# The pool of small tiles moves from above to below the weights' and the large buffers' pools

## The chip, the cores and the metric

The kernel runs on one core of a Trainium2 chip. The metric is the time of one execution in microseconds (us) on the device; lower is better. Engines are named as in the profile: PE (TensorE matmuls), PEld (the weight loads of TensorE), DVE (VectorE), ACT (ScalarE), POOL (GpSimd) and SP (SyncE, which issues transfers).

## The reference

Two layers over a residual stream of 1024 tokens by 1024 features, batch 1, all in float32. Cut to what matters here:

```
for i in range(2):
    h = rms_norm(x, norm_mix_g[i])
    u_conv, q, k, v, g = split(h @ w_in[i])             # 1024 -> 3072
    conv_out = conv_module(u_conv, ...)                 # 31 taps, layer norm, silu
    ret = chunkwise_retention(q, k, v, positions)       # 4 heads of 128, chunks of 128
    ret_out = silu(g) * group_norm(ret)
    x = x + concat([conv_out, ret_out]) @ w_out[i]
    h = rms_norm(x, norm_ffn_g[i])
    x = x + square(relu(h @ w_ff1[i])) @ w_ff2[i]       # 1024 -> 4096 -> 1024
    h = rms_norm(x, norm_ple_g[i])
    x = x + sigmoid(h @ w_ple_gate[i]) * (p[i] @ w_ple_proj[i])
return rms_norm(x, final_norm_g)
```

## The kernel before, in words

Activations lie feature-major: a tile holds 128 features on the partitions and 512 tokens (half of the sequence) along the row, so a wide matmul has a stationary operand of 128x128 and a moving operand of 128x512, one PSUM bank. Each float32 operand is split into a high and a low part (`split`, lines 219 to 221: ACT rounds to the high part, DVE subtracts for the low one), and each product is three matmuls, high by high, high by low and low by high (`mm3`, lines 250 to 254). So lines 252, 253 and 254 are nearly all of PE's work, and every group of matmuls in the profile comes three times with the same count.

The stages of a layer: the input projections with the convolution, the retention and the output projection (`proj_ab` to `w_out`), in which the stationary operand is a weight tile (`w_hi`, `w_lo`) and the moving one an activation tile (`h`), or the other way round for q, k and v (`proj_tok`); the first feed-forward projection, half of it directly (`ff1_half`, line 596) and half by a seven-product scheme on sums of weights and of activations (`ff1_pair`, line 649); the second one by the same scheme (`ff2_pairs`, line 733) with a direct remainder (`ff2`, line 810); and the per-layer embedding (`ple_proj`, `ple`).

Where tiles lie is set by the order in which pools are opened (lines 77 to 95). Pools of the left side are stacked: first `const`, then in `__init__` `stage`, `w_hi`, `w_lo`, `h`, `tmp` and `small`, which stay for the whole run, and on top of them the pools of a stage, which are opened and closed in `run` with `stage_pools`: `gen`, `conv_acc`, `ret`, `ctmp`, `rtmp`, `u` (line 887), `at`, `hx`, `s_hi`, `s_lo`, `ft` (lines 951 and 952), `form`, `acc` (line 982) and `pp`, `pr` (line 991). Normalisation has its own pools on the right side, from the other end of the memory.

Bytes per partition: `stage`, `w_hi` and `w_lo` hold 2 tiles of 4096 each, `h` 8 of 8192, `tmp` 2 of 2048. The stage pools that feed matmuls have tiles of 2048, 4096 or 8192 (`u` with 2168 comes last on its stack). All these are multiples of 512. The pool `small` has ten names with three slots each; a slot is rounded up to 32 bytes, so nine names take 96 bytes each, and `gn_st` (96 bytes a slot) takes 288: 9 x 96 + 288 = 1152 bytes, which is 2 x 512 + 128.

Which operands lie where in the wide matmuls (below: "lower pools" for `stage`, `w_hi`, `w_lo`, `h`, `tmp`, "upper pools" for those of a stage):

- `h` with `w_hi`, `w_lo`: both in the lower pools (all projections, `ff1_half`, one product of five in `ff1_pair`, part of `ff2_pairs`).
- `hx` or `form` with `s_hi`, `s_lo`: both in the upper pools.
- `h` with `s_hi`, `s_lo`; `hx`, `form` or `pp` with `w_hi`, `w_lo`: one in each.

A run of `ff1_pair` is five products of four 128-row blocks, 60 matmuls, in this order: `sa` by `t2`, `sa` by `t1` (into `ps_ret`), `sb` by `t3`, `sb` by `q22`, `w` by `t4`. Here `sa`, `sb` are pairs of `s_hi`, `s_lo`; `t3` lies in `hx`, the other activation forms in `h`. There are 16 such runs in each layer. `ff2_pairs` runs 7 blocks x 4 pairs in each layer, each seven products of two 128-row blocks, 42 matmuls. The forms of the next block come back from memory by POOL's transfers (`fetch`, line 709) into a ring of slots in `h`, `hx` and `form`, each after PE has read the slot's last occupant, and are split by ACT and DVE (`ready`, line 715). At the start of a block `begin` (lines 738 to 745) computes `p` and copies it on ACT (line 744), and the next matmuls into `p` wait for that copy.

The order of each engine's instructions is the order of the program text with priorities (`background`); it does not depend on where a tile lies.

Of the kernel before, what the change touches and what calls it, by code (L numbers as in the profile page):

```python
# [72 lines left out]
class _Trunk:  # L73
    def __init__(self, ctx, tc, x, xT, pT, pos, wts, vecs, convw, tabs, outT):
        self.tc, self.nc = tc, tc.nc
        self.x_tok, self.xT, self.pT, self.pos, self.wts = x, xT, pT, pos, wts
        self.vecs, self.convw, self.tabs, self.outT = vecs, convw, tabs, outT
        pool = lambda name, bufs, **kw: ctx.enter_context(tc.tile_pool(name=name, bufs=bufs, **kw))
        psum = bass.MemoryType.PSUM
        self.const = pool("const", 1)  # L80
        self.pools = {
            "stage": pool("stage", 2),
            "w_hi": pool("w_hi", 2),
            "w_lo": pool("w_lo", 2),
            "h": pool("h", 8),
            "tmp": pool("tmp", 2),
            "small": pool("small", 3),
            "ps_mm": pool("ps_mm", 5, space=psum),
            "ps_ret": pool("ps_ret", 2, space=psum),
            "ps_aux": pool("ps_aux", 1, space=psum),  # L90
        }

        self.small([P, 1], "pad")
        self.right = ctx.enter_context(ExitStack())
        self.norm_pools()
        self.dram = pool("dram", 1, space=bass.MemoryType.DRAM)
        self.low = {}
# [987 lines left out]
```

## Time and profile before

| | |
|---|---|
| median of 3 runs | 2378.33 us (2377.74 to 2378.8) |
| time of the profiled execution | 2378.69 us |
| its span, first to last instruction | 2376.7 us |
| PE busy | 2314.1 us (97%) |
| DVE / ACT / POOL busy | 1857.8 (78%) / 1267.6 (53%) / 231.9 us (10%) |
| mean granted TensorE clock | 0.994 |

PE's records are pipelined: one matmul of 512 columns is shown for some 0.39 us, while the next starts about 0.23 us after it. So neither the busy time nor the mean duration of a matmul says how fast PE goes; the distance from one start to the next does, and it is read from the timeline of PE, or from the number of matmuls in a stretch in which PE never idles.

### The profile page before, as it was taken

What the parts mean: (1) busy time and instruction counts of PE and PEld (TensorE: products, weight loads), DVE (VectorE), ACT (ScalarE), POOL (GpSimd) and SP (SyncE); (2) the same over time, 40 slices, a digit from 0 to 9 for tenths busy, and PEclk for the clock granted to TensorE, in tenths of its full rate; (3) what the DMA queues carried; (4) which work ended last, traced back from release to release, by engine and by line L of the source; (5) the groups of instructions that cost most, each with busy time, mean ns of one, the idle gap of its engine ahead of it and who ended that gap; (6) DMA issues with size and microseconds to landing.
All of it is one profiled execution on the core that took longest, in us unless ns stands there. A gap on an engine that the chain in (4) does not pass through costs nothing.

```text
span 2376.7 us, 29537 instructions
## 1 busy us (share of the span) xinstructions
PE 2314.1 (97%) x10548; PEld 1886.0 (79%) x10548; DVE 1857.8 (78%) x3262; ACT 1267.6 (53%) x2090; POOL 231.9 (10%) x364
## 2 busy tenths in 40 slices
PE   8999999999999999999999999999999999999998
PEld 7887887778887878788888888777788877777887
DVE  8999997376666677878999889845766667777788
ACT  5335237365556676736542352464655567676454
POOL 1000011001221101000000100100022111010000
PEclk9999999999999999999999999999999999999999
DMA  7644544666666444422265454555566654343324
GB/s 271 194 160 150 172 149 163 227 199 204 219 233 239 141 151 138 155 72 88 89 195 180 149 171 156 175 196 187 191 218 233 237 194 164 126 162 120 89 80 151
DMA packets 119171, 403.29 MB, mean 170 GB/s; under 512 B 13216, under 2 KB 21408, under 8 KB 119024
## 3 DMA queue, kind: packets, MB, share of 16 engines
q1 hardware_dynamic: 64032, 220.75, 30.5%
q0 software_dynamic: 43472, 157.59, 18.6%
q10 hardware_dynamic: 11520, 23.07, 2.6%
q8 instruction: 82, 1.34, 0.2%
q14 instruction: 65, 0.53, 0.1%
HBM read 295.46 MB, written 105.91 MB: 169 GB/s over the span
## 4 chain that ended last, share of the span: by engine, by line
PE 63%; issue 20%; DVE 8%; DMA 3%; POOL 3%; ACT 3%; POOLq 0%; DVEq 0%; ACTq 0%
PE ps_mm L252 19%; PE ps_mm L253 19%; PE ps_mm L254 19%; DVE conv_acc L411 2%; PE ps_ret L252 2%; PE ps_ret L254 2%; PE ps_ret L253 2%; POOL h L712 1%; DMA stage<-in_wts_dram 1%; DVE w_lo L221 1%; DVE h L221 1%; POOL gn_rs L546 1%; DMA w_lo<-low 1%; DMA h<-forms 1%; DVE ntmp L277 0%
## 5 line engine op out<-in xcount | busy, mean ns | idle before, releaser
L252 PE MATMUL ps_mm<-h,w_hi 128*128 128x512 f32 (+1 forms) x1584 | 615.2, 388 | 8.6 <-ACT w_hi L241 4.2
L254 PE MATMUL ps_mm<-h,w_lo 128*128 128x512 f32 (+1 forms) x1584 | 611.5, 386 | 2.9 <-DMA w_lo<-low 2.7
L253 PE MATMUL ps_mm<-h,w_hi 128*128 128x512 f32 (+1 forms) x1584 | 613.0, 387 | 0.0
L220 ACT CAST w_hi<-stage 128x1024 fp32r<-128x1024 f32 (+2 forms) x240 | 226.6, 944 | 300.1 <-PE ps_mm L253 169.7
L252 PEld LDWEIGHTS ps_mm<-h,w_hi 128*128 128x128 f32 x1584 | 299.2, 189 | 69.3 <-ACT w_hi L241 6.1
L254 PEld LDWEIGHTS ps_mm<-h,w_lo 128*128 128x128 f32 x1584 | 299.3, 189 | 62.8 <-DMA w_lo<-low 3.5
L253 PEld LDWEIGHTS ps_mm<-h,w_hi 128*128 128x128 f32 x1584 | 299.6, 189 | 56.1
L411 DVE SCALAR_TENSOR_TENSOR conv_acc<-u,cw,conv_acc 128x512 f32<-128x512 f32 x480 | 334.6, 746 | 0.9
L221 DVE TENSOR_TENSOR w_lo<-stage,w_hi 128x1024 fp32r<-128x1024 f32 (+2 forms) x240 | 261.1, 1088 | 51.0 <-ACT w_hi L220 50.3
L252 PE MATMUL ps_mm<-h,s_hi 128*128 128x512 f32 x400 | 158.9, 397 | 4.5 <-ACT ps_mm L661 4.5
L253 PE MATMUL ps_mm<-h,s_hi 128*128 128x512 f32 x400 | 158.5, 396 | 0.0
L254 PE MATMUL ps_mm<-h,s_lo 128*128 128x512 f32 x400 | 158.0, 395 | 0.0
L252 PE MATMUL ps_mm<-w_hi,h 128*128 128x512 f32 x384 | 150.6, 392 | 0.0
L253 PE MATMUL ps_mm<-w_lo,h 128*128 128x512 f32 x384 | 150.3, 391 | 0.0
L254 PE MATMUL ps_mm<-w_hi,h 128*128 128x512 f32 x384 | 150.2, 391 | 0.0
L241 ACT CAST w_hi<-stage 128x1024 fp32r<-128x1024 f32 x64 | 67.5, 1054 | 154.4 <-PE ps_mm L253 80.7
L270 ACT ACTIVATE ntmp<-x 128x256 f32<-128x256 f32 x208 | 81.1, 413 | 84.7 <-DVE ntmp L277 32.2
L252 PE MATMUL ps_ret<-h,s_hi 128*128 128x512 f32 x272 | 110.0, 405 | 16.5 <-ACT ps_mm L744 14.4
L221 DVE TENSOR_TENSOR s_lo<-ft,s_hi 128x1024 fp32r<-128x1024 f32 x64 | 78.4, 1225 | 52.7 <-ACT s_hi L220 52.7
L221 DVE TENSOR_TENSOR h<-h 128x1024 fp32r<-128x1024 f32 x76 | 92.6, 1222 | 30.8 <-ACT h L220 30.4
L254 PE MATMUL ps_ret<-h,s_lo 128*128 128x512 f32 x272 | 108.4, 398 | 0.0
L253 PE MATMUL ps_ret<-h,s_hi 128*128 128x512 f32 x272 | 108.0, 397 | 0.0
(267 smaller groups left out, 4310.1 us busy)
## 6 DMA issues: line engine op xcount, KB each, us to landing
stage<-in_wts_dram SPq DMA_DIRECT2D x336, 512.0 KB, 4.2
forms<-ft POOLq DMA_DIRECT2D x88, 512.0 KB, 6.2
low<-w_lo POOLq DMA_DIRECT2D x64, 512.0 KB, 5.2
w_lo<-low SPq DMA_DIRECT2D x64, 512.0 KB, 3.3
h<-forms POOLq DMA_DIRECT2D x62, 512.0 KB, 6.0
early<-at ACTq DMA_DIRECT2D x32, 512.0 KB, 4.4
at<-early POOLq DMA_DIRECT2D x30, 512.0 KB, 4.2
hx<-forms POOLq DMA_DIRECT2D x18, 512.0 KB, 5.7
```

What stands on the lines that cost most here:

```text
L220: self.nc.scalar.copy(hi, src)
L221: self.nc.vector.tensor_sub(lo, src, hi.bitcast(F32))
L241: self.nc.scalar.copy(hi, st)
L252: mm(ps, lhsT=wh, rhs=xh, start=start, stop=False)
L253: mm(ps, lhsT=wh, rhs=xl, start=False, stop=False)
L254: mm(ps, lhsT=wl, rhs=xh, start=False, stop=stop)
L270: square = lambda k, out: nc.scalar.activation(out, self.x[k][h][:, cs], AF.Square)
L411: nc.vector.scalar_tensor_tensor(acc, u[:, j:j + HT], w(j), acc, ALU.mult, ALU.add)
L546: nc.gpsimd.tensor_tensor(rs, rs, self.npow[:, 0:HEADS], ALU.pow)
L712: self.nc.gpsimd.dma_start(out=f[1].bitcast(F32), in_=src)
```

## The change

The pool `small` is opened first, just above `const`. It has the same tiles and the same size, so the pools `stage`, `w_hi`, `w_lo`, `h` and `tmp` lie 1152 bytes higher than before; the upper pools, which start where `tmp` or `small` ended, keep their places, as do `const` and the right side. Relative to the upper pools, the lower pools thus move by 1152 bytes, which is 128 modulo 512. No instruction is added, removed or moved. (Line numbers below the diff grow by one.)

```
         self.const = pool("const", 1)
+
+
         self.pools = {
+            "small": pool("small", 3),
             "stage": pool("stage", 2),
             "w_hi": pool("w_hi", 2),
             "w_lo": pool("w_lo", 2),
             "h": pool("h", 8),
             "tmp": pool("tmp", 2),
-            "small": pool("small", 3),
             "ps_mm": pool("ps_mm", 5, space=psum),
             "ps_ret": pool("ps_ret", 2, space=psum),
             "ps_aux": pool("ps_aux", 1, space=psum),
         }
-
         self.small([P, 1], "pad")
```

## Rows read from the trace of the kernel before

**Rows 1.** The page: its first line, and PE of its part 1.

```profile
span 2376.7 us, 29537 instructions
...
PE 2314.1 (97%) x10548; PEld 1886.0 (79%) x10548; DVE 1857.8 (78%) x3262; ACT 1267.6 (53%) x2090; POOL 231.9 (10%) x364
```

**Rows 2.** Busy time by stretch: the columns, a loop of `ff1_pair`, a projection stretch.

```profile
core 0: us, PE busy (x) PEld busy (x) DVE busy (x) ACT busy (x) POOL busy (x), PEclk, DMA share, GB/s
...
600.00:700.00 100.00, 100.00 (x434) 81.28 (x433) 66.44 (x92) 57.20 (x87) 19.25 (x29) 1.00 0.69 230
...
1250.00:1300.00 50.00, 50.00 (x222) 41.43 (x221) 49.61 (x83) 10.64 (x11) 4.80 (x9) 1.00 0.63 195
```

**Rows 3.** Timeline of PE, 1250 to 1295 us: first and last of 197 matmuls.

```profile
1249.74 0.39 PE L253 MATMUL ps_mm<-w_lo,h 128*128 128x512 f32 x1
...
1294.16 0.39 PE L254 MATMUL ps_mm<-w_hi,h 128*128 128x512 f32 x1
```

**Rows 4.** Timeline of PE, 600 to 615 us: one run of `ff1_pair`, 60 matmuls.

```profile
600.49 0.39 PE L252 MATMUL ps_mm<-hx,s_hi 128*128 128x512 f32 x1
...
602.10 0.39 PE L253 MATMUL ps_mm<-hx,s_hi 128*128 128x512 f32 x1
...
603.23 0.40 PE L252 MATMUL ps_mm<-h,s_hi 128*128 128x512 f32 x1
...
606.02 0.40 PE L252 MATMUL ps_mm<-h,w_hi 128*128 128x512 f32 x1
...
608.79 0.40 PE L252 MATMUL ps_mm<-h,s_hi 128*128 128x512 f32 x1
...
614.37 0.39 PE L252 MATMUL ps_mm<-hx,s_hi 128*128 128x512 f32 x1
```

**Rows 5.** Timeline of PE, 2250 to 2272 us: two matmuls 90 starts apart.

```profile
2250.10 0.40 PE L254 MATMUL ps_mm<-pp,w_lo 128*128 128x512 f32 x1
...
2271.09 0.39 PE L252 MATMUL ps_mm<-h,w_hi 128*128 128x512 f32 x1
```

**Rows 6.** Groups of PE's instructions, shapes apart; count, then busy us, mean ns.

```profile
L252 PE MATMUL ps_mm<-h,w_hi 128*128 128x512 f32 x1488 | 587.0, 394 | 8.2 <-ACT w_hi L241 4.2 <-ACT w_hi L220 3.8
...
L252 PE MATMUL ps_mm<-h,s_hi 128*128 128x512 f32 x400 | 158.9, 397 | 4.5 <-ACT ps_mm L661 4.5
...
L252 PE MATMUL ps_ret<-h,s_hi 128*128 128x512 f32 x272 | 110.0, 405 | 16.5 <-ACT ps_mm L744 14.4 <-ACT s_hi L220 1.8 <-ACT ps_mm L770 0.3
...
L252 PE MATMUL ps_mm<-hx,w_hi 128*128 128x512 f32 x64 | 25.6, 400 | 0.0
...
L252 PE MATMUL ps_mm<-pp,w_hi 128*128 128x512 f32 x64 | 24.9, 395 | 0.0
...
L252 PE MATMUL ps_mm<-form,w_hi 128*128 128x512 f32 x32 | 12.6, 394 | 0.0
...
L252 PE MATMUL ps_ret<-hx,w_hi 128*128 128x512 f32 x16 | 6.3, 392 | 0.0
```

**Rows 7.** Waits of PE, whole run: who for whom, us, times, longest.

```profile
PE ps_ret L252 <- ACT ps_mm L744: 16.9, 12, 4.8
```

**Rows 8.** Timeline of all engines, 829 to 837 us, at a block's start.

```profile
829.26 0.72 POOL L712 DMA_DIRECT2D h<-early  x1 [0.86 <-PE ps_mm L254]
...
835.40 1.05 ACT L220 CAST h<-h 128x1024 fp32r<-128x1024 f32 x1 [1.11 <-DMA h<-early]
836.35 0.58 ACT L744 COPY ps_mm<-ps_ret 128x512 f32<-128x512 f32 x1
...
836.98 0.50 PE L252 MATMUL ps_ret<-h,s_hi 128*128 128x512 f32 x1 [0.86 <-ACT ps_mm L744]
```

**Rows 9.** Groups of DVE's instructions, 520 to 1075 us, shapes apart.

```profile
L589 DVE TENSOR_TENSOR ft<-ft,stage 128x512 f32<-128x512 f32 x15 | 10.3, 686 | 0.0
...
L695 DVE TENSOR_TENSOR ft<-ft 128x512 f32<-128x512 f32 x14 | 9.6, 685 | 0.0
```

**Rows 10.** The page, part 6: transfers, KB each, us from issue to landing.

```profile
h<-forms POOLq DMA_DIRECT2D x62, 512.0 KB, 6.0
...
hx<-forms POOLq DMA_DIRECT2D x18, 512.0 KB, 5.7
```

More of the change, by code (lines that the diff above doesn't have):

```diff
@@ L81, in __init__ @@
         self.pools = {
+            "small": pool("small", 3),
             "stage": pool("stage", 2),
@@ L86, in __init__ @@
             "tmp": pool("tmp", 2),
-            "small": pool("small", 3),
             "ps_mm": pool("ps_mm", 5, space=psum),
```

## The prediction

> **What bounds the kernel now.** I began with the page's first part: PE is busy for 2314.1 of 2376.7 us [rows 1]. No other engine comes near, and the time that PE stands still is about 63 us in all. A busy PE is not yet a PE at its best pace, so the next view is the distance between the starts of its matmuls, at full clock and in stretches in which PE never idles (both hold in [rows 2]).
>
> In a projection stretch, where `h` and the weights lie in the lower pools, 196 starts take 1294.16 - 1249.74 = 44.42 us, 226.6 ns each [rows 3], although DVE is busy there for 49.61 of 50 us [rows 2]. In `ff1_pair` PE is just as busy but slower: 434 matmuls are seen in 100 us [rows 2], and one run of 60 takes 614.37 - 600.49 = 13.88 us, 231.3 ns each [rows 4]. Here the products can be told apart. I call a product unlike when one operand is in the lower and one in the upper pools: from the sizes of the pools, their tiles are then 128 bytes apart modulo 512; in the others they are 0 apart. In order [rows 4]:
>
> - `hx` with `s` (both upper, alike): the first 7 starts take 1.61 us, 230 ns each, the next 5 take 1.13 us, 226 ns;
> - `h` with `s` (unlike): 12 starts in 2.79 us, 232.5 ns;
> - `h` with `w` (both lower, alike), right behind an unlike product: 12 in 2.77 us, 231 ns;
> - `h` with `s` twice (unlike): 24 in 5.58 us, 232.5 ns.
>
> `pp` with `w`, unlike too, needs 20.99 us for 90 starts, 233.2 ns [rows 5]. So an unlike product costs some 6 ns a matmul at any length, and an alike one comes down to 226 to 227 ns, but only some matmuls after the unlike one has ended. It is not where the two tiles lie as such: both lower is as fast as both upper. And it is hardly distance: `pp` begins 1152 + 4096 bytes above the end of `h`, so it is about as far from `w` as the last tiles of `h` are.
>
> **The change part by part.** It adds and removes no instruction, no wait and no transfer, and moves no step past another in any queue. What it does is to make all unlike products alike.
>
> *The unlike matmuls.* Each group comes three times [rows 6]: 3 x (400 + 272) of `h` with `s`, 3 x (64 + 16) of `hx` with `w`, 3 x 64 of `pp`, 3 x 32 of `form`: 2544 in all, of 9600 wide ones.
>
> *`ff1_pair`.* 32 runs (16 in each layer) of 13.88 us [rows 4] would take 60 x 226.6 ns = 13.60 us each: 32 x 0.28 = 9.0 us. This has both the 36 unlike matmuls of a run and the slow recovery in its 24 alike ones.
>
> *`ff2_pairs` and `ff2`.* Unlike there are 2544 - 32 x 36 - 192 = 1200, at 232.5 - 226.6 = 5.9 ns: 7.1 us. Their alike ones recover as well: 7 x 4 x 2 x 42 + 384 = 2736 matmuls less 1200, at 228.3 - 226.6 = 1.7 ns (228.3 being the mean of the 12 alike starts of `hx` in [rows 4]): 2.6 us.
>
> *`pp`.* 192 x (233.2 - 226.6) = 1.3 us.
>
> Together 20.0 us. Two things come off. A mixed stretch doesn't reach 226.6 throughout: after each wait some matmuls pass before the pace is back, and I leave 0.4 ns on each of the 32 x 60 + 2736 + 192 = 4848 matmuls (the 222 matmuls of the projection stretch, with 0.39 us of overlap at its edges, make 50.39 / 222 = 227.0 [rows 2]): 1.9 us. And part of the gain is taken up by waits. The largest is for ACT's copy at line 744, 16.9 us in 12 cases [rows 7]. At one of these, POOL issues a fetch at 829.26, released by PE; ACT's split of it starts at 835.40, the copy stands behind it in ACT's queue at 836.35, and PE goes on at 836.98 [rows 8]. That chain is a transfer and two ACT steps long whatever PE's pace, and in its 7.7 us PE runs some 30 matmuls, so up to 30 x 5 ns = 0.15 us of gain turns into a longer wait, 12 times: 1.8 us. Sum: 20.0 - 1.9 - 1.8 = 16.3 us.
>
> *What else is touched.* DVE and ACT read and write the moved tiles. A DVE add with one operand in each half takes 686 ns, one with both in the upper pools 685 ns [rows 9], so I take nothing for them. In `ff1_pair` DVE is busy 66 and ACT 57 of 100 us [rows 2], which covers a pace of PE 2% higher with ease. Transfers into `h` change their place: `h<-forms` lands after 6.0 us, `hx<-forms`, which doesn't move, after 5.7 [rows 10]. If place were the cause, the waits of [rows 7] would shrink by up to 12 x 0.3 = 3.6 us; the other way they would grow by as much. I take 0, since nothing ties the 0.3 us to the place, and keep both ends.
>
> *The size at its ends.* At least: the unlike matmuls only come down to what alike ones show beside them in the same loop now, 228.3 ns, 2544 x 4.2 = 10.7 us, less 1.8: 9 us. At most: the whole 20.0 and some of the transfers' gain, 21 to 22 us.
>
> The profiled execution took 2378.69 us, 0.36 above the median of the runs. 2378.33 - 16.3 = 2362.0 us.
>
> *A rule against it.* Behind the 232.5 and 226.6 ns stands a rule of the Trainium skill that says otherwise: the page "TensorE: Matmul & The Clock Gate", Part 2, What happens when you issue a matmul, states that PE has two independent read ports, and that "loading the next tile's weights doesn't steal SBUF read bandwidth from the running matmul". By that rule no placement could matter and the sum would be 0. The trace speaks against it, unless the 6 ns come from something else; that is the first rival.
>
> **The rivals.**
>
> *Something else that goes with the unlike products.* Not the offset modulo 512 but, say, the mixing of an upper with a lower pool or the way these products follow each other slows them. All tiles of the lower pools move together, by 1152 bytes only, so nothing would change: 2378. For it: `h` with `w` in `ff1_pair` is at 231 ns though alike [rows 4]. Against it: that product follows an unlike one, its like is at 226.6 elsewhere [rows 3], and `pp`, next to the lower pools, is slow for 90 starts on end [rows 5]. Of this kind is also that the stack of pools might not come out as I count it. Chance 0.08.
>
> *The second loop gives its gain back.* PE in `ff2_pairs` is fed through slots that it frees itself, and the chain of [rows 8] could hold more often than 12 times once PE is faster, so that only `ff1_pair` and `pp` count: 9.0 + 1.3 = 10.3, 2368. Against it: there are 56 runs of 42 matmuls and only 12 such waits, all at a block's start. Chance 0.12.
>
> *Slower: the lower pools now collide with the other engines.* What is slow could be two readers of one residue, with DVE in the place of the weight load. In the projection stages DVE works in the upper pools (the convolution's sums, the rotary tiles); until now these are 128 apart from what PE reads, and then they are not. If that cost PE its 6 ns on the 3 x 1488 = 4464 matmuls of `h` with `w` [rows 6], it would be 26.3 us against 16.3 gained: 2388. It decides from 16.3 / 5.9 ns = 2760 of these matmuls on. Against it: `hx` with `s` runs at 226 ns while DVE and ACT write into `ft` and `at`, all of them in the upper pools [rows 4]; but DVE is less busy there. Chance 0.04.
>
> **How the numbers follow.** The forecast, a gain of 9 to 21 us, has 0.76. The range goes from 2357, the upper size, to 2370, which takes in the lower size and the second rival. It leaves out the other two, 0.12, and some mishaps of size. A measurement of this kernel can tell about 0.2%, 4.8 us, from no change. Faster by more: the forecast and the second rival, 0.88. Within: the first rival, 0.08. Slower by more: 0.04.
>
> **What would show it.** In the new profile the run of `ff1_pair` should take 13.6 to 13.7 us instead of 13.88, 100 us of it should show 441 or 442 matmuls instead of 434, and `pp` should come at 227 ns; the projection stretch should stay at 227. PE's wait for line 744's copy (then one line further down) should grow by 1 to 2 us in the same 12 places. If `h` with `s` stays at 232 ns, the offset is not the cause; if the spacing falls and the time doesn't, the gain went into waits, and these must have grown by as much; if the projection stretch slows down, it is the third rival.

## The result and the profile after

The changed kernel takes 2366.11 us (median of 4, 2362.04 to 2369.27) where the kernel before takes 2378.51: a ratio of 0.9947, interval [0.993, 0.9965], 12.4 us less. Run again (e5 below) it was 2363.24 against 2379.38, 0.9933 [0.992, 0.9945], 16.1 us less. Forecast were 16.3 us.

The page of the changed kernel, first line and PE of part 1, answers to [rows 1] (line numbers are one higher from here on):

```profile
span 2365.7 us, 29537 instructions
...
PE 2296.4 (97%) x10548; PEld 1884.2 (80%) x10548; DVE 1856.7 (78%) x3262; ACT 1266.6 (54%) x2090; POOL 232.0 (10%) x364
```

PE is busy for 17.7 us less, the span is only 11.0 us shorter: PE's idle time went from 62.6 to 69.3 us. Nothing else moved; DVE and ACT are within 1.1 us of before. Busy time by stretch, columns as in [rows 2]:

```profile
600.00:700.00 100.00, 100.00 (x443) 82.80 (x442) 67.08 (x93) 57.70 (x88) 18.96 (x28) 1.00 0.69 235
1250.00:1300.00 50.00, 50.00 (x224) 41.40 (x223) 49.62 (x88) 11.13 (x12) 4.79 (x9) 1.00 0.61 183
```

443 matmuls in 100 us of `ff1_pair` in place of 434; with the 0.39 us of overlap at the edges that is 100.39 / 443 = 226.6 ns each, where it was 231.3. The projection stretch, which was alike before, keeps its pace (50.39 / 224 = 225 ns; three short matmuls are among them). One run of `ff1_pair` in the timeline of PE, from `h` with `s` to the same product of the next run, as in [rows 4]:

```profile
602.28 0.39 PE L253 MATMUL ps_mm<-h,s_hi 128*128 128x512 f32 x1
...
605.00 0.39 PE L253 MATMUL ps_mm<-h,w_hi 128*128 128x512 f32 x1
...
607.72 0.39 PE L253 MATMUL ps_mm<-h,s_hi 128*128 128x512 f32 x1
...
615.88 0.39 PE L253 MATMUL ps_mm<-h,s_hi 128*128 128x512 f32 x1
```

60 matmuls in 13.60 us, each 12 of them in 2.72 us whatever the product. The second loop, for which the prediction had 9.7 of its 20.0 us, shows the same. From 770 to 830 us, in which PE never idles in either kernel, the kernel before and the changed one have:

```profile
770.00:830.00 60.00, 60.00 (x261) 48.71 (x261) 41.81 (x64) 38.90 (x59) 6.22 (x11) 1.00 0.41 132
...
770.00:830.00 60.00, 60.00 (x267) 49.67 (x266) 42.72 (x64) 41.25 (x62) 7.31 (x13) 1.00 0.47 151
```

That is 60.39 / 261 = 231.4 ns before and 60.39 / 267 = 226.2 after. Of `pp`, which took 233.2 ns [rows 5], 12 starts late in the stretch:

```profile
2255.85 0.39 PE L253 MATMUL ps_mm<-pp,w_hi 128*128 128x512 f32 x1
...
2258.57 0.39 PE L253 MATMUL ps_mm<-pp,w_hi 128*128 128x512 f32 x1
```

2.72 us again, 226.7 ns. So the pace came down as forecast. What came back is in PE's waits. In the whole run, as in [rows 7]:

```profile
PE ps_ret L253 <- ACT ps_mm L745: 21.4, 12, 4.7
...
PE ps_ret L254 <- DVE h L222: 1.5, 2, 0.8
...
PE ps_ret L253 <- ACT h L221: 1.1, 2, 0.7
```

The wait for ACT's copy of `begin` grew from 16.9 to 21.4 us in the same 12 places: two at the starts of the second loop, which did not grow (4.80 and 4.69 us before, 4.71 and 4.69 after), and ten at the starts of later blocks. Two kinds of wait are new, twice each, 2.6 us together, for the first forms of the second loop. Together 7.1 us; the idle time as a whole grew by 6.7. (The new ones do not belong to the offset: e2 and e10 below, which keep an offset, have waits for such a split of 0.7 and 1.3 us, and e5, the changed kernel again, has none.) The longest of the ten waits at blocks' starts, in the timeline of all engines, is to be held beside [rows 8]:

```profile
2109.17 0.72 POOL L713 DMA_DIRECT2D h<-early  x1 [0.83 <-PE ps_mm L255]
...
2117.10 1.04 ACT L221 CAST h<-h 128x1024 fp32r<-128x1024 f32 x1 [2.57 <-DMA h<-early]
2118.05 0.58 ACT L745 COPY ps_mm<-ps_ret 128x512 f32<-128x512 f32 x1
...
2118.68 0.50 PE L253 MATMUL ps_ret<-hx,s_hi 128*128 128x512 f32 x1 [2.74 <-ACT ps_mm L745]
```

It is the chain of [rows 8], but 7.9 us from the fetch to the split where that was 6.1: here the transfer took longer, so PE's pace is not all of this wait. ACT stands for 2.57 us on a transfer, the copy stands behind it, and PE waits 2.74 us for the copy. What ACT waits for is an early split of a form of the next block (by the program text that of `ready(2 * g - 2)`, line 776 before; counted from the loop's start, its fetch is that block's), and that block starts some 39 us later. The text has this split behind the copy; in ACT's queue it stands ahead of it. So the order of an engine's instructions is not simply that of the text, as was told ahead of the prediction, and a split can be moved back behind the copy (e6).

### The profile page after: what moved, and what is told of

Same layout as the page of the kernel before. It is cut to its first block, busy times and chain, and to the rows that moved or that the text cites. A ratio compares the mean times of both kernels' runs of the same rounds, so it can differ in the third digit from the quotient of the medians.

```text
span 2365.7 us, 29537 instructions
## 1 busy us (share of the span) xinstructions
PE 2296.4 (97%) x10548; PEld 1884.2 (80%) x10548; DVE 1856.7 (78%) x3262; ACT 1266.6 (54%) x2090; POOL 232.0 (10%) x364
## 4 chain that ended last, share of the span: by engine, by line
PE 63%; issue 20%; DVE 8%; DMA 4%; POOL 3%; ACT 3%; POOLq 0%; DVEq 0%; ACTq 0%
PE ps_mm L253 19%; PE ps_mm L255 18%; PE ps_mm L254 18%; DVE conv_acc L412 2%; PE ps_ret L253 2%; PE ps_ret L254 1%; PE ps_ret L255 1%; DMA stage<-in_wts_dram 1%; POOL h L713 1%; DVE w_lo L222 1%; POOL gn_rs L547 1%; DVE h L222 1%; DMA w_lo<-low 1%; DMA h<-forms 1%; DMA h<-early 1%
## 5 line engine op out<-in xcount | busy, mean ns | idle before, releaser
L255 PEld LDWEIGHTS ps_mm<-h,w_lo 128*128 128x128 f32 x1584 | 299.6, 189 | 62.6 <-DMA w_lo<-low 4.1
L253 PE MATMUL ps_mm<-h,s_hi 128*128 128x512 f32 x400 | 155.8, 390 | 4.9 <-ACT ps_mm L662 4.9
L254 PE MATMUL ps_mm<-h,s_hi 128*128 128x512 f32 x400 | 155.6, 389 | 0.0
```

The lines of the kernel that those rows point to most:

```text
L253: mm(ps, lhsT=wh, rhs=xh, start=start, stop=False)
L254: mm(ps, lhsT=wh, rhs=xl, start=False, stop=False)
L255: mm(ps, lhsT=wl, rhs=xh, start=False, stop=stop)
```

## The experiments

**e1 to e4 and e8, e10: is it the offset?** Each leaves the instructions as they are and moves pools.

**e1: new order, offset 128 as before.**

```
+            "gap": pool("gap", 1),                 # behind "tmp"
...
-        self.small([P, 1], "pad")
+        self.pools["gap"].tile([P, 32], F32, name="gap")
```

> The small pool stays below, but a gap of 128 bytes is left between the lower and the upper pools (and the small pool's pad tile is dropped), so the offset between the two is 128 modulo 512 again. If the offset is the cause: the time of before, 2377 to 2380 us, a run of ff1_pair in 13.9 us, PE busy for 2314 us. If the order of the pools, or the place of the lower pools as such, is the cause: it stays with the changed kernel, 2362 to 2369 us, 13.6 us a run and 2296 us busy.

2381.49 us, 1.0008 [0.9999, 1.0017] of before. Its stretch of `ff1_pair`:

```profile
600.00:700.00 100.00, 100.00 (x435) 81.27 (x434) 66.41 (x92) 57.06 (x86) 19.07 (x29) 1.00 0.69 230
```

The old pace in the new order: while the offset stays at 128, neither the order nor the move upwards changes anything.

**e2: 64 bytes apart.** The changed kernel with a `gap` tile of [P, 16] behind `tmp` (the pad tile stays).

> As the changed kernel, with a gap of 64 bytes between the lower and the upper pools. If only an offset of 0 modulo 512 is fast: 231 ns a matmul in ff1_pair and 2374 to 2380 us. If the slowdown is worked out in steps coarser than 64 bytes: the changed kernel's 226.7 ns and 2362 to 2369 us. If it grows with the offset: half way, 229 ns and about 2372 us.

2380.90 us, 1.0006 [0.9997, 1.0015].

```profile
600.00:700.00 100.00, 100.00 (x433) 80.97 (x432) 66.48 (x92) 56.97 (x86) 18.95 (x28) 1.00 0.68 229
```

100.39 / 433 = 231.8 ns: half the offset costs as much as the whole.

**e3: old order, alike by size.**

```
             "small": pool("small", 3),
+            "small2": pool("small2", 2),
...
-        self.small([P, 1], "pad")
...
-            sh = self.small([P, 1], "ln_sh")
+            sh = self.pools["small2"].tile([P, 1], F32, name="ln_sh")
```

> The order of the pools of before, with the small pool made 128 bytes smaller (no pad tile, one name with two slots in place of three), so that it takes 1024 bytes and the pools below and above it are alike, both at the other residue. If the offset is the cause: as the changed kernel, 2362 to 2369 us, PE busy for 2296 us, a run of ff1_pair in 13.6 us. If the order or the absolute place is the cause: as before, 2378 us.

2364.42 us, 0.9935 [0.9919, 0.9952].

```profile
600.00:700.00 100.00, 100.00 (x442) 82.79 (x442) 67.10 (x93) 57.77 (x89) 19.22 (x29) 1.00 0.71 235
```

The gain without the change's order, and with all tiles at the residue that the lower pools had before. It is the offset between the two, not where either lies.

**e4: `h` apart from the weights.**

```
             "w_lo": pool("w_lo", 2),
+            "small": pool("small", 3),
             "h": pool("h", 8),
             "tmp": pool("tmp", 2),
-            "small": pool("small", 3),
```

> The small pool lies between the weights' pools and h, so that h is alike with s_hi, s_lo, hx, and unlike with w_hi, w_lo. By the offset: the 2016 matmuls of h with s become fast, the 4464 of h with w, the 1152 of the token-major projections and 288 more into ps_ret become slow, the 528 of hx, form and pp with w stay slow. So 3888 more at 5.9 ns, 23 us of spacing, less what the waits take up: 2393 to 2403 us, and 232 to 233 ns a matmul between 1250 and 1300 us where it was 226.6. If mixing stage pools with the others is what costs, or something else that goes with those products: 2378 us, and 226.6 ns there.

2393.86 us, 1.0056 [1.0041, 1.0071], the low end of what was expected.

```profile
600.00:700.00 100.00, 100.00 (x439) 82.17 (x438) 69.06 (x98) 58.68 (x90) 19.53 (x29) 1.00 0.66 222
1250.00:1300.00 50.00, 50.00 (x216) 40.20 (x216) 48.14 (x78) 9.83 (x12) 4.81 (x9) 1.00 0.63 187
```

The slowness goes where the offset goes: the projection stretch falls to 50.39 / 216 = 233.3 ns, which no placement tried before had touched, and `ff1_pair` gets faster. That rules out anything that belongs to the feed-forward products themselves. The size that was expected, 23 us of spacing, was too large: PE's busy time grew by 2329.9 - 2314.1 = 15.8 us, and its idle time did not grow (62.6 before, 62.0 here), so no wait took the rest. For one thing, the count took every `h` with `w` as fast before, but in `ff1_pair` those took 231 ns already [rows 4]; the rest of the difference is open.

**e8: 256 bytes apart.** The new order with a `gap` tile of [P, 64], no pad tile, and `ln_sh` and `norm_rs` in a pool of two slots, to make room.

> The new order with the lower and the upper pools 256 bytes apart modulo 512 (a gap of 256 bytes; the pad tile is dropped and two names of the small pool get two slots in place of three). If 512 bytes are the period: unlike products stay slow, 230 to 233 ns, and 2376 to 2382 us. If 256 bytes are: 226.7 ns in ff1_pair and the changed kernel's time.

2365.89 us (two runs), 0.9942 [0.9922, 0.9961].

```profile
600.00:700.00 100.00, 100.00 (x443) 82.81 (x442) 67.14 (x95) 58.17 (x88) 18.95 (x28) 1.00 0.70 235
```

As fast as alike. Modulo 512 is more than is needed.

**e10: 32 bytes apart.** As e2 with a `gap` tile of [P, 8].

> The changed kernel with a gap of 32 bytes between the lower and the upper pools. 128 and 64 apart were slow, 256 and 0 fast. If every offset that is not a multiple of 256 is slow: 231 to 232 ns in ff1_pair and 2376 to 2382 us. If the steps that matter are 64 bytes: 226.7 ns and 2361 to 2368 us.

2382.05 us, 1.0013 [1.0002, 1.0023].

```profile
600.00:700.00 100.00, 100.00 (x434) 81.26 (x433) 66.53 (x93) 57.29 (x87) 19.71 (x29) 1.00 0.69 230
```

Offsets of 0 and 256 bytes are fast, 32, 64 and 128 slow, all by 4 to 5 ns on the mean of the stretch. Other offsets were not tried.

**e5: the changed kernel again.**

> The changed kernel itself, run again beside the next two so that they share a chip and its runs of before. 12 to 16 us under the kernel before of the same rounds, if its first figure of 12.4 us holds.

16.1 us less, as told above: PE is busy for 2298.4 of 2365.5 us, with 21.7 us of waits for the copy. Both figures for the changed kernel hold; single executions of either kernel lie up to some 5 us from their median.

**e6 and e7: where did the rest go?** The same edit on the kernel after and on the kernel before:

```
             copy(q, p)
+            self.mark = nc.cur_bb.bb.instructions[-1]
             return e, p, q, ws[0], ws[1]
...
-                    self.ready(2 * g - 2)
+                    with self.tc.issue_after(self.mark):
+                        self.ready(2 * g - 2)
...
-                    self.ready(2 * g - 1)
+                    with self.tc.issue_after(self.mark):
+                        self.ready(2 * g - 1)
```

> The changed kernel with the early splits of a block's forms (the two calls of ready for g = 1 and 2) put behind the copy of begin on ACT, so that the copy never stands behind a split that waits for a transfer. If the missing 6 us went into that copy's wait: PE's wait for it falls from 21.4 to some 10 us (the two of 4.7 us where the second loop starts stay), and the time is 8 to 11 us under the changed kernel's. If the chain of transfer, split and product holds PE anyway: the changed kernel's time within 3 us, and other waits of PE, for a split of h, hx or form, in place of the copy's.

> The same edit on the kernel before, with the small pool where it was. If the gain was given back at that copy: 5 to 8 us under the kernel before, the copy's wait at 9 to 10 us in place of 16.9, and the changed kernel with this edit 17 to 19 us under this one, which is the 18.8 us that the spacing of the matmuls fell by. If the gain went elsewhere: 12 us between the two, as without the edit.

e6: 2350.86 us, 0.9878 [0.9865, 0.9891], 12.4 us under the changed kernel beside it. PE's waits in e6:

```profile
PE ps_ret L253 <- ACT ps_mm L745: 9.5, 2, 4.8
```

The ten waits at blocks' starts are gone, the two at the loop's starts are left, and the wait fell by 21.7 - 9.5 = 12.2 us. The median fell by about as much, but the profiles do not put it all down to this wait: from e5 to e6 PE's idle time fell by 10.5 us (67.1 to 56.6) and its busy time by 5.9 (2298.4 to 2292.5).

e7: 2362.55 us, 0.9928 [0.9916, 0.9941], 16.8 us under before where 5 to 8 were expected, and only 11.7 us over e6 where 17 to 19 were. Its copy's wait is 8.7 us, a little under the 9 to 10 expected. By its own expectation, 12 us between the two means that the missing gain had not gone into that copy. Something else could have helped e7, and the one view in which it stood out was the granted clock around the starts of the two loops (the third column from the end). That was tried by running both again.

**e11 and e12: the two once more.**

> The kernel before with the copy of begin ahead of the early splits, once more, for its clock. The first time it took 2362.6 us where 2371 to 2373 was expected, and its profile shows granted clocks of 1.00, 0.95, 1.00 and 0.95 around the two starts of the feed-forward loops of both layers, where the changed kernel with the same edit shows 0.94, 0.90, 0.93 and 0.90. If the shorter waits keep the clock up by themselves: the same clocks and 2360 to 2365 us. If it was this profile's luck: clocks near 0.94 and 0.90, and some 2366 to 2370 us in its profiled execution.

> The changed kernel with that edit, once more. If its lower clock goes with its way of running: 0.90 again in the second loop's starts and 2349 to 2352 us, 11 to 13 us under the run beside it. If it was luck: clocks of 0.95 to 1.00 there in some executions, and 2343 to 2352 us.

e11: 2365.99 us, 0.994 [0.9922, 0.9959]; e12: 2350.09 us, 0.9876 [0.9852, 0.9901]; 15.9 us apart. The granted clock in e7, the first time, by stretch:

```profile
515.00:545.00 30.00, 26.76 (x116) 21.09 (x115) 19.35 (x26) 18.38 (x27) 3.25 (x5) 1.00 0.51 172
740.00:775.00 35.00, 30.49 (x126) 24.36 (x125) 24.79 (x33) 26.09 (x38) 5.21 (x9) 0.95 0.63 234
1680.00:1705.00 25.00, 21.72 (x94) 16.99 (x93) 15.46 (x21) 15.54 (x23) 1.61 (x3) 1.00 0.45 153
1900.00:1935.00 35.00, 30.84 (x128) 24.68 (x128) 23.38 (x31) 24.09 (x34) 7.44 (x13) 0.95 0.70 260
```

and in e11, the same kernel:

```profile
515.00:545.00 30.00, 26.78 (x108) 21.05 (x107) 18.65 (x25) 17.24 (x27) 3.17 (x5) 0.94 0.47 159
740.00:775.00 35.00, 30.02 (x118) 23.51 (x117) 24.67 (x32) 23.21 (x34) 5.89 (x11) 0.90 0.67 244
1680.00:1705.00 25.00, 21.66 (x94) 16.96 (x93) 14.57 (x19) 15.40 (x23) 1.09 (x2) 1.00 0.53 171
1900.00:1935.00 35.00, 30.28 (x120) 23.97 (x119) 21.16 (x26) 23.86 (x34) 8.40 (x15) 0.90 0.75 270
```

The clock of e7 didn't come back with the same kernel; its span of 2360.4 became 2363.5.

In the second pair the spans differ by 2363.5 - 2347.8 = 15.7 us, PE's busy time by 2308.1 - 2291.9 = 16.2 us, and the idle times are alike (55.4 and 55.9). In the first pair these are 11.3 and 12.6 us (55.3 and 56.6). So with the copy's wait out of the way nearly all that PE's busy time falls by arrives in the time. But the change is not worth more than with the wait: 11.7 and 15.9 us in these two pairs, 12.4 and 16.1 without the edit. That the wait had taken the missing microseconds is thus not shown. Nor are the 17 to 19 us reached; e12's clock is also below e11's in the third stretch:

```profile
1680.00:1705.00 25.00, 22.10 (x89) 17.71 (x90) 16.37 (x21) 12.45 (x20) 2.70 (x4) 0.93 0.51 173
```

And the edit is worth more on the kernel before (14 to 17 us) than its waits (8 us). A part of that is busy time, which is less by 8.9 us on the unlike side (the mean of e7 and e11 beside that of the four profiles without the edit, in the table of the next section) and by 5.1 on the alike side (e6 and e12). After a wait PE needs some matmuls to find its pace again: six starts take 838.49 - 836.98 = 1.51 us before and 834.38 - 832.89 = 1.49 after, some 250 ns each, in an alike product as in an unlike one. By these numbers ten such waits make about 1 us (an estimate); how the rest divides wasn't tried.

**e9: the start of the second loop too.** e6, with the copy of `begin` at higher priority and the splits of forms 3 to 6 behind it:

```
-                        self.ready(2, 3)
+                        self.ready(2)
...
-            copy(q, p)
+            with self.background(-300):
+                copy(q, p)
...
-                    self.ready(*((4, 5, 6) if j == 0 else (6,)))
+                    with self.tc.issue_after(self.mark):
+                        self.ready(*((3, 4, 5, 6) if j == 0 else (6,)))
```

> As the changed kernel with the early splits behind the copy of begin, and in addition, where the second loop starts, the splits of forms 3 to 6 behind that copy too (form 3 was split before it). PE waits there twice for 4.7 to 4.8 us, and the granted clock falls to 0.5 right after it, so that matmuls start 427 ns apart. If those waits are ACT's queue alone: they fall to 1 to 2.5 us, 5 to 7 us in both layers, and if the clock falls because of the wait, it stays at 1.0 there and gives 3 to 6 us more: 2338 to 2346 us. If the waits hang on something behind the copy (the split form, the transfer): a wait for a split takes their place, and 2350 us as without this edit.

2348.49 us, 0.9878 [0.9862, 0.9895] of before: no different from e6.

```profile
PE ps_ret L253 <- ACT w_hi L221: 7.5, 2, 3.9
```

At the first of these two waits the timeline has:

```profile
749.18 0.81 ACT L221 CAST w_hi<-stage 128x768 fp32r<-128x768 f32 x1
...
750.04 0.79 PE L253 MATMUL ps_ret<-h,w_hi 128*128 128x512 f32 x1 [3.89 <-ACT w_hi L221]
```

A miss, by the way told last in the expectation: PE no longer waits for the copy there, but for a split of weights. The edit had changed PE's order too: six more matmuls of `h` with `w` now stand ahead of those of `h` with `s` that e6 runs at this point, and they need the split that ACT starts at 749.18 us. ACT has no gap from 746.10 us to the copy, which runs at 751.05 where it ran at 751.49 in e6, and the clock fell as before (0.90 at both starts). e6, e9 and e12 are the fastest versions, 1.2% under the kernel before, and cannot be told apart.

## Why the prediction was right

*The pace.* Step by step as forecast. `ff1_pair`: 13.60 us a run, the number of the sum. Its products and `pp` come at 226.6 to 226.7 ns, with no slow recovery left in the loop. PE's busy time: 20.0 - 1.9 = 18.1 us forecast, 17.7 measured. (The 9600 wide matmuls of the prediction include 288 of 256 columns; no term rests on them.) The offset was the right cause (e1, e3), and the slowness follows it to other products (e4), so the first rival fell. The rule that the prediction cited from the Trainium skill's "TensorE: Matmul & The Clock Gate", Part 2, What happens when you issue a matmul, by which a weight load takes no bandwidth from the running matmul, would have made the sum 0 as it was read there; PE's busy time fell by 17.7 us. The runs show that the pace depends on the offset of the two operands; why it does, and whether the weight load is what slows the matmul, they do not show. The third rival, the lower pools colliding with the other engines, would have slowed the projection stretch, which stayed as it was.

*The waits.* This term was sized at 1.8 us for the copy, 0.15 us in each of 12 places; two of these are the loop's starts, where the wait is of another kind and did not grow. The first profile has 4.5 us there and 2.6 us of new waits at the second loop's start, for which the prediction had no term. One profile of each kernel is thin for that. Eight profiles lie on the two sides of the offset: unlike before, e1, e2, e10, alike after, e3, e5, e8. Means over four, from their pages:

| | span | PE busy | idle | wait for the copy |
|---|---|---|---|---|
| unlike | 2380.4 | 2315.5 | 64.9 (62.6 to 66.0) | 18.2 (16.9 to 19.4) |
| alike | 2364.7 | 2297.3 | 67.4 (64.9 to 69.3) | 20.4 (17.2 to 21.7) |
| alike less unlike | -15.7 | -18.2 | +2.5 | +2.2 |

So the copy's wait is 2.2 us longer on the mean, near the 1.8 of the sum, and the kernel before happened to be profiled at its shortest. But the two groups overlap (16.9 to 19.4 and 17.2 to 21.7), and the transfers of the two chains shown differ by 1.8 us, so the agreement in this size may be luck. The 16.3 us forecast stand beside 15.7 here and 12.4 and 16.1 in the two timed comparisons. The mechanism of the second rival is there, a chain of a transfer and ACT's steps, but in the places that the kernel had already; it doesn't hold the loop, whose pace came down (267 matmuls where 261 were).

*Nothing for DVE, ACT and the transfers.* DVE's busy time is 1.1 us less, ACT's 1.0. `h<-forms` lands after 6.0 us as before, `hx<-forms`, which didn't move, after 5.9 where it was 5.7 [rows 10]: place had no part in it.

*What the prediction didn't see.* Ten of the twelve waits hang on a split that isn't needed yet. The chain was read in [rows 8] down to the split of `h`, but not asked whose form it was. That question was worth 12 us on the changed kernel and 14 to 17 on the kernel before, about as much as the change itself.

## What to carry to other kernels

When PE is busy all the time, read the distance between the starts of its matmuls product by product and hold it beside where the two operands lie: here a moving and a stationary tile that lay 128 bytes apart modulo 256 cost 6 to 7 ns of 227 on every such matmul of 512 columns, 32 and 64 bytes slowed the same loop by as much, and ordering or padding pools added no instruction. A matmul that comes faster shortens the time only where PE doesn't wait; so list its waits as well and ask of each what stands ahead of the releaser in its queue, and whether that is needed yet.

## What the runs showed of the hardware that was not expected

- Offsets of 0 and 256 bytes between the lower and the upper pools give 226.6 to 227.1 ns (442 or 443 matmuls in 100 us of `ff1_pair`), 32, 64 and 128 give 231 to 232 (433 to 435). A half or a quarter of the offset is no better than the whole.
- A long wait costs PE more than its length. In e6, behind the wait of 4.79 us at the second layer's loop, the timeline of PE reads:

```profile
1910.18 0.79 PE L253 MATMUL ps_ret<-h,s_hi 128*128 128x512 f32 x1 [4.79 <-ACT ps_mm L745]
...
1912.48 0.63 PE L255 MATMUL ps_ret<-h,s_lo 128*128 128x512 f32 x1
1912.90 0.63 PE L253 MATMUL ps_mm<-h,w_hi 128*128 128x512 f32 x1
1913.33 0.63 PE L254 MATMUL ps_mm<-h,w_hi 128*128 128x512 f32 x1
1913.76 0.63 PE L255 MATMUL ps_mm<-h,w_lo 128*128 128x512 f32 x1
```

 The starts from 1912.48 to 1913.76 are 427 ns apart (3 in 1.28 us), 512 columns at 1.2 GHz: the lower of the two levels. The mean granted clock from 1900 to 1935 us was 0.90 in before, after, e6 and e9 to e12 and 0.95 in e7, whose two waits of this kind make 8.7 us together, where they make 9.5 in e11. A shorter wait is not needed for the higher clock: e5, the changed kernel itself, has it behind a wait of 4.73 us, where the first profile of the same kernel has 0.90 behind 4.69:

```profile
1916.08 0.51 PE L253 MATMUL ps_ret<-h,s_hi 128*128 128x512 f32 x1 [4.73 <-ACT ps_mm L745]
...
1900.00:1935.00 35.00, 30.23 (x125) 24.21 (x124) 26.73 (x34) 26.39 (x38) 6.28 (x11) 0.95 0.69 256
```

 So the clock in this stretch varies between executions of one kernel; what decides it is open. For the kernel of e7 and e11, the span was 3 us longer with the lower clock.
